# Low parts of 78 weight tiles computed in earlier feed-forward stages, stored to DRAM and loaded again

## The chip, the cores and the metric

The kernel runs on one core of a Trainium2 chip. The time is that of one execution on the device, in microseconds (us); three executions of the kernel before were taken.

## The reference

The model is a two-layer decoder trunk on 512 tokens of width 1024, in float32. Each layer adds half a SwiGLU feed-forward block (hidden width 2816), then a mixer, then half of a second feed-forward block. The mixer of layer 0 is the RWKV-7 time mixing (16 heads of 64, a recurrence over the tokens), that of layer 1 a causal convolution module.

```python
for i in range(DEPTH):
    x = x + 0.5 * swiglu(rms_norm(x, g[i, 0]), w_gate[i, 0], w_up[i, 0], w_down[i, 0])
    h = rms_norm(x, g[i, 1])
    x = x + (rwkv7_time_mix(h, ...) if i % 2 == 0 else conformer_conv(h, ...))
    x = x + 0.5 * swiglu(rms_norm(x, g[i, 2]), w_gate[i, 1], w_up[i, 1], w_down[i, 1])
return rms_norm(x, final_norm)
```

## The kernel before

All large products are products of a weight block of 128 x 128 with activations, channels on partitions and tokens along the free axis. For accuracy each float32 operand is split into a high part, its cast to the format F32R, and a low part, the rest. A product is then three matrix products: high by high, high by low, low by high (`mmw`).

The weights come as one stream of tiles, `wst`, eight blocks (512 KB) to a tile, in the order in which the steps of the program take them. `wfetch` handles tile i: SP loads it into `wr` (three buffers), ScalarE casts it to the high part `wh`, VectorE subtracts to get the low part `wl` (two buffers each). There are 446 tiles. `wblk` hands out the blocks and fetches one tile ahead.

`program()` lists the steps: `gu` and `dn` are the two halves of a feed-forward block, `f0` to `f3` the four blocks. Between `f0` and `f1` lies the time mixing: `rw` and `rx` norm the input, `kk`, `k`, `r`, `v`, `lora`, `w2`, `g1` are projections, `a` and `b` the two stages of a head group's recurrence, `w` the output projection. Between `f2` and `f3` lies the convolution: `cin` (input projection and gate), `tap` (31 taps, shared by VectorE in `dwa`, ScalarE and GpSimd in `dwt`, and TensorE in `dwx`, whose shifted inputs go through DRAM as `hd` and come back as `hr`), `cln` (layer norm), `co` (output projection). Some steps work on half of the tokens, 256 columns, some on all 512.

The steps don't issue instructions. They record them in `Sched`, which afterwards issues them by a list schedule: from modelled costs each engine takes, of the instructions whose operands and buffers are there, the one that can start first, and among equals the one that is oldest in program order (the casts of weights count as 10 us older, `LEAD`). SP, which issues the loads and stores, is scheduled in the same way. Working tiles of 2 KB a partition come from a pool of 80 slots. Where TensorE would idle for long, the schedule adds products that nothing reads (`warm`). In the profile all recorded instructions have one line, L617, where `emit` issues them; they are told apart by their tiles.

Up to 8 transfers of a queue are under way at a time: each waits for the semaphore of the eighth before it.

Of the kernel before, what the change touches and what calls it, by code (L numbers as in the profile page):

```python
# [12 lines left out]
F32 = mybir.dt.float32  # L13
F32R = mybir.dt.float32r
I32 = mybir.dt.int32
AF = mybir.ActivationFunctionType
ALU = mybir.AluOpType

P = 128
T = 512  # L20
D = 1024
NB = D // P
# [3 lines left out]
WT = 8  # L26
CH = 64
# [58 lines left out]
HALF3 = 1  # L86

# [5 lines left out]
def program():  # L93
    """The steps in program order (their weight blocks are streamed in this order). A step
    with a half h works on tokens 0-255 (0), 256-511 (1) or on all of them (2)."""
# [6 lines left out]
    def ffn(f, j0=0, mid=None):  # L102
        """From hidden block j0 on; with mid (lists of steps), the last sums run on one half of
        the tokens, then on the other half with one of the lists before each."""
# [74 lines left out]

PROG = program()  # L180

# [40 lines left out]
class Sched:  # L222
    """Records engine instructions in program order and issues them in the order of a
    list schedule: each engine takes the oldest instruction whose operands are there."""
# [50 lines left out]
    def after(self, eng, ap, n=1):  # L275
        """The next n instructions of an engine also wait for the writers of ap."""
        self.extra.append([eng, ap, n])
# [61 lines left out]
    def lag(a, b):  # L339
        """From the end of an instruction on a to the start of its reader on b."""  # L340
# [41 lines left out]
    def order(self):  # L382
# [38 lines left out]
        def fits(op, e):  # L421
            """Time at which the op's new tiles have room on engine e, or None."""
# [36 lines left out]
        def free(op, e):  # L459
            """Time from which no other engine's earlier instruction is at the op's banks."""  # L460
# [167 lines left out]
class Net:  # L628
    def __init__(self, ctx, tc, xT, wst, cvec, cst, dwv, outT):
# [17 lines left out]
        self.wtiles = {}  # L647
        self.wnext = 0
# [30 lines left out]
    def warm(self):  # L679
        """A product that nothing reads: keeps the tensor engine's clock up."""  # L680
# [6 lines left out]
    def wfetch(self):  # L687
# [8 lines left out]
        l = self.s.tile(self.wp, [P, WT, P], F32R, f"wl{i}", "wl", WB)  # L696
        self.s.lead = LEAD
# [4 lines left out]
        self.wtiles[i] = (h, l)  # L702

# [23 lines left out]
    def projs(self, ps, parts):  # L727
        """A projection of parts of the tokens: (columns, operand) each."""
# [17 lines left out]
    def turn(self, out, src):  # L746
        """Transposes each [P, P] block of src."""
# [4 lines left out]
    def scratch(self, name):  # L752
        """DRAM tile for a [P, NC, CH] array, strided so that the diagonal 16-blocks of a
        head lie at one stride: views (whole, low half, high half, blocks of head 0, 1)."""
# [6 lines left out]
    def rsqrt(self, y, v, n, tight=False):  # L761
        """y = v ** -0.5 elementwise on a small tile."""
# [37 lines left out]
    def sq_block(self, b, nm, h=2):  # L800
        """Sums the squares of x over its blocks but the last, on tokens of half h."""
# [891 lines left out]
```

## Time and profile before

| | |
|---|---|
| median of three runs | 2296.72 us (2292.44 to 2300.92) |
| the profiled execution | 2300.92 us, span 2300.8 us |
| TensorE products busy | 2214.8 us, 96% of the span |
| VectorE busy | 1368.3 us, 59% |
| ScalarE busy | 912.2 us, 40% |
| GpSimd busy | 608.6 us, 26% |
| low parts `wl` on VectorE | 561.5 us in 448 instructions |
| bytes moved | 261.96 MB, 114 GB/s on average |

Times in the profile count from the first instruction. PE is TensorE, PEld its loading of weights, DVE VectorE, ACT ScalarE, POOL GpSimd, SP the engine that issues most transfers. A view by windows gives each engine's busy time in a stretch, and the share of full speed that TensorE's clock was granted there. A view of waits names what ended an engine's idle time. The stages lie about so: first feed-forward block 0 to 390, time mixing 390 to 990 (with parts of the second feed-forward block in its gaps), rest of the second block to 1313, third block to 1681, convolution to about 1900 (with the start of the fourth block), fourth block to the end.

### The profile page before, as it was taken

The page shows a single profiled execution, that of the slowest core. Times are in us where ns is not written, and L with a number is a line of the kernel's source. Part 1 is how long each engine was busy: PE and PEld are TensorE (multiplying, and loading weights), DVE is VectorE, ACT ScalarE, POOL GpSimd, SP SyncE. Part 2 cuts the span into 40 slices and gives each one's busy share as a digit, 9 for nine tenths or more (in the row PEclk, how much of TensorE's full clock was granted, in tenths as well). Part 3 has the DMA queues.
Part 4 walks back from the last instruction along what each step waited for, and adds up shares of the span by engine and source line. Part 5 has one row for each costly group of instructions (what it writes and reads, how often), then busy time and mean ns, then how long its engine had stood idle before and what let it go on. Part 6 is the DMA issues. An engine that isn't in the chain of part 4 may idle for free. (4 is left out here: it accounts for less than half of the span.)

```text
span 2300.8 us, 37819 instructions
## 1 busy us (share of the span) xinstructions
PE 2214.8 (96%) x15256; PEld 1903.0 (83%) x15256; DVE 1368.3 (59%) x2201; ACT 912.2 (40%) x1506; POOL 608.6 (26%) x582
## 2 busy tenths in 40 slices
PE   9999999899989999999999999999997799999998
PEld 7888888667778788899999888888875589998898
DVE  5333347876796786566433433334479998753454
ACT  4222235546633453344322322123344555532343
POOL 2100113543352161022011112011157733311111
PEclk9999999899998997999999999999999999999999
DMA  4333336123224233256533333333334635653465
GB/s 154 97 96 101 97 124 183 46 75 90 60 64 115 76 101 98 76 166 182 156 93 92 92 98 99 92 101 93 92 111 124 164 98 166 179 147 93 126 184 158
DMA packets 120464, 261.96 MB, mean 114 GB/s; under 512 B 47072, under 2 KB 59744, under 8 KB 120288
## 3 DMA queue, kind: packets, MB, share of 16 engines
q1 hardware_dynamic: 86624, 254.29, 37.5%
q10 hardware_dynamic: 33664, 5.25, 1.3%
q8 instruction: 120, 1.97, 0.4%
q14 instruction: 56, 0.46, 0.1%
HBM read 249.96 MB, written 9.54 MB: 113 GB/s over the span
## 5 line engine op out<-in xcount | busy, mean ns | idle before, releaser
L617 ACT CAST wh<-wr 128x1024 fp32r<-128x1024 f32 (+1 forms) x448 | 467.3, 1045 | 994.3 <-issue 365.3
L617 DVE TENSOR_TENSOR wl<-wr,wh 128x1024 fp32r<-128x1024 f32 (+1 forms) x448 | 561.5, 1255 | 254.3 <-ACT wh L617 245.9
L617 DVE SCALAR_TENSOR_TENSOR dwa<-ch,dw,dwa 128x256 f32<-128x256 f32 (+10 forms) x176 | 115.3, 697 | 0.1
L617 POOL TENSOR_TENSOR f1ss<-f1ss,n1rs 128x256 f32<-128x256 f32 (+1 forms) x33 | 47.2, 1433 | 235.6 <-ACT f1ss L617 235.5
L617 POOL TENSOR_TENSOR f0ss<-f0ss,n0rs 128x512 f32<-128x512 f32 x22 | 38.6, 1756 | 258.0 <-ACT f0ss L617 258.0
L617 POOL TENSOR_TENSOR f2ss<-f2ss,n2rs 128x512 f32<-128x512 f32 x22 | 39.0, 1773 | 255.8 <-ACT f2ss L617 255.8
L617 POOL TENSOR_TENSOR f3ss<-f3ss,n3rs 128x256 f32<-128x256 f32 (+1 forms) x33 | 49.3, 1495 | 182.5 <-ACT f3ss L617 182.5
L617 PE MATMUL f3u<-f_h,wl 128*128 128x256 f32 (+1 forms) x264 | 84.7, 321 | 2.1 <-DVE wl L617 2.1
L617 PE MATMUL f3g<-f_h,wl 128*128 128x256 f32 (+1 forms) x264 | 84.8, 321 | 1.5 <-DVE wl L617 1.4
L617 PE MATMUL f3u<-f_l,wh 128*128 128x256 f32 (+1 forms) x264 | 84.5, 320 | 0.0
L617 PE MATMUL f3g<-f_l,wh 128*128 128x256 f32 (+1 forms) x264 | 84.3, 319 | 0.0
L617 PE MATMUL f3g<-f_h,wh 128*128 128x256 f32 (+1 forms) x264 | 84.2, 319 | 0.0
L617 PE MATMUL f3u<-f_h,wh 128*128 128x256 f32 (+1 forms) x264 | 84.2, 319 | 0.0
L617 POOL TENSOR_TENSOR dwt<-dwt,dwt 128x256 f32<-128x256 f32 (+5 forms) x80 | 72.9, 923 | 2.7
L617 PE MATMUL f0g<-f_2h,wh 128*128 128x512 f32 x176 | 70.2, 399 | 2.5 <-ACT wh L617 2.5
L617 PE MATMUL f0g<-f_2l,wh 128*128 128x512 f32 x176 | 70.1, 399 | 1.9 <-DVE f_2l L617 1.9
L617 PE MATMUL f2g<-f_2h,wl 128*128 128x512 f32 x176 | 69.4, 394 | 0.0
L617 PE MATMUL f0u<-f_2h,wh 128*128 128x512 f32 x176 | 69.4, 394 | 0.0
L617 PE MATMUL f0g<-f_2h,wl 128*128 128x512 f32 x176 | 69.4, 394 | 0.0
L617 PE MATMUL f0u<-f_2l,wh 128*128 128x512 f32 x176 | 69.4, 394 | 0.0
L617 PE MATMUL f2u<-f_2l,wh 128*128 128x512 f32 x176 | 69.4, 394 | 0.0
L617 PE MATMUL f2g<-f_2l,wh 128*128 128x512 f32 x176 | 69.3, 394 | 0.0
(1509 smaller groups left out, 7048.7 us busy)
## 6 DMA issues: line engine op xcount, KB each, us to landing
wr<-wst SPq DMA_DIRECT2D x444, 512.0 KB, 3.6
hr<-hd SPq DMA_DIRECT2D x64, 64.5 KB, 3.8
hr<-hd SPq DMA_DIRECT2D x64, 59.2 KB, 2.0
x<-xT SPq DMA_DIRECT2D x8, 256.0 KB, 6.1
xspill<-x SPq DMA_DIRECT2D x8, 256.0 KB, 4.4
dl<-Gb ACTq DMA_DIRECT2D x16, 128.0 KB, 2.1
t<-dt ACTq DMA_DIRECT2D x8, 256.0 KB, 3.4
xr<-xspill SPq DMA_DIRECT2D x8, 256.0 KB, 6.0
```

Source lines behind the costliest of these rows:

```text
L617: self.tc.keep_in_program_order(getattr(eng, m)(*op.args, **op.kw))
```

## The change

78 tiles are taken out of the usual path: the tiles 77 to 124, which the time mixing takes first, and 300 to 329, the convolution's. For each of them a new step `ps` is put into the program earlier: the 48 of the time mixing spread over the first feed-forward block from its third hidden block on, the 30 of the convolution over the third feed-forward block (`early`; `WCOUNT` counts the weight blocks of a step). `step_ps` loads the raw tile in two halves of 256 KB (`pw`), casts each on ScalarE (`ph`), subtracts on VectorE in place, and stores the low part to DRAM (`lo`). When such a tile comes up later, `wfetch` loads the raw tile as before and casts it on ScalarE, but loads the low part from DRAM into `wl` in place of VectorE's subtraction. Nothing else of the computation changes. (In the new file the docstrings and comments are gone, so the line of the recorded instructions is L658.)

```diff
+PS = (48, 30)
...
+def early(prog, of, to, at, end, n, skip=0):
+    pos = [0]
+    for s in prog:
+        pos.append(pos[-1] + WCOUNT(*s))
+    lo, hi = -(-pos[of] // WT), pos[to] // WT
+    tiles = list(range(lo, hi))[skip:skip + n]
+    a, b = pos[at], pos[end]
+    where = {}
+    for k, i in enumerate(tiles):
+        p = a + (b - a) * (k + 0.5) / len(tiles)
+        j = at
+        while pos[j + 1] <= p:
+            j += 1
+        where.setdefault(j, []).append(("ps", i))
+    out = []
+    for j, s in enumerate(prog):
+        out += [s] + where.get(j, [])
+    return out, set(tiles)
...
 PROG = program()
+PRE = set()
+PROG, t_ = early(PROG, find(PROG, "rw", 1), find(PROG, "prep", 1, 1), 3, find(PROG, "rw", 0), PS[0])
+PRE |= t_
+PROG, t_ = early(PROG, find(PROG, "conv"), find(PROG, "cln", 1), find(PROG, "prep", 2) + 2, find(PROG, "conv"), PS[1])
+PRE |= t_
...
         l = self.s.tile(self.wp, [P, WT, P], F32R, f"wl{i}", "wl", WB)
+        if i in self.lows:
+            nc.sync.dma_start(l.bitcast(F32), self.lows[i].rearrange("p (a b) -> p a b", b=P))
+            self.s.lead = LEAD
+            nc.scalar.copy(h, raw)
+            self.s.lead = 0.0
+            self.wtiles[i] = (h, l)
+            return
...
+    def step_ps(self, i):
+
+        nc = self.nc
+        self.lows[i] = d = self.dp.tile([P, WT * P], F32, name=f"lo{i}")
+        for k in range(WT * P // T):
+            c = slice(k * T, k * T + T)
+            n = T // P
+            w = self.slot(f"pw{i}_{k}", F32R)
+            h = self.slot(f"ph{i}_{k}", F32R)
+            nc.sync.dma_start(w.bitcast(F32).rearrange("p (a b) -> p a b", b=P), self.wst[i][:, k * n:k * n + n])
+            nc.scalar.copy(h, w.bitcast(F32))
+            nc.vector.tensor_tensor(w, w.bitcast(F32), h.bitcast(F32), ALU.subtract)
+            nc.sync.dma_start(d[:, c], w.bitcast(F32))
```

How the schedule places the new instructions shows in the built order. The number after a name's letters is the tile, the last number a buffer's.

On SP in the first feed-forward block, before: nothing but raw tiles, one after the other.

```order
L617 DMA wr7_154<-wst 128x1024
L617 DMA wr8_158<-wst 128x1024
L617 DMA wr9_166<-wst 128x1024
L617 DMA wr10_170<-wst 128x1024
L617 DMA wr11_178<-wst 128x1024
L617 DMA wr12_182<-wst 128x1024
```

Now, from raw tile 8 on:

```order
L658 DMA wr8_168<-wst 128x1024
L658 DMA lo87_275<-pw87_0_276 128x512
L658 DMA lo88_292<-pw88_0_293 128x512
L658 DMA pw101_0_435<-wst 128x512
L658 DMA lo78_158<-pw78_1_161 128x512
L658 DMA wr9_181<-wst 128x1024
L658 DMA lo89_309<-pw89_0_310 128x512
L658 DMA lo90_314<-pw90_0_315 128x512
L658 DMA lo79_175<-pw79_1_178 128x512
L658 DMA pw101_1_437<-wst 128x512
L658 DMA lo91_326<-pw91_0_327 128x512
L658 DMA lo80_192<-pw80_1_195 128x512
```

Between two raw tiles stand the loads of tiles that are wanted some 90 tiles later, and the stores of low parts. Up to and with raw tile 16 SP's queue has 78 `pw` loads, 62 `lo` stores and 17 raw tiles.

On VectorE in the convolution, where the gate of channel block 4 (`ctg4`) is scaled, before:

```order
L617 TENSOR_TENSOR ctg4_2_2685<-cg4_2_2680,ncrs_2593 128x512
L617 TENSOR_TENSOR wl311_2699<-wr311_2697,wh311_2698 128x1024
L617 SCALAR_TENSOR_TENSOR dwa3_2667<-ch3_2666,dw_2562,dwa3_2667 128x246
L617 SCALAR_TENSOR_TENSOR ch4_2686<-cta4_2_2684,vec_72,ctg4_2_2685 128x512
L617 SCALAR_TENSOR_TENSOR dwa3_2667<-ch3_2666,dw_2562,dwa3_2667 128x245
L617 TENSOR_SCALAR dwa4_2687<-ch4_2686,dw_2562,vec_72 128x256
```

Now:

```order
L658 TENSOR_TENSOR ctg4_2_3075<-cg4_2_3070,ncrs_2983 128x512
L658 SCALAR_TENSOR_TENSOR dwa3_3057<-ch3_3056,dw_2952,dwa3_3057 128x256 x2
L658 SCALAR_TENSOR_TENSOR ch4_3076<-cta4_2_3074,vec_72,ctg4_2_3075 128x512
L658 SCALAR_TENSOR_TENSOR dwa3_3057<-ch3_3056,dw_2952,dwa3_3057 128x256
L658 TENSOR_SCALAR dwa4_3077<-ch4_3076,dw_2952,vec_72 128x256
```

The subtraction `wl311` between the taps `dwa` is gone; the taps of block 3 that stood around it now stand around `ch4` alone.

On SP in the time mixing, before:

```order
L617 DMA wr94_850<-wst 128x1024
L617 DMA wr95_860<-wst 128x1024
L617 DMA wr96_866<-wst 128x1024
L617 DMA wr97_894<-wst 128x1024
L617 DMA wr98_901<-wst 128x1024
```

Now:

```order
L658 DMA wr96_1106<-wst 128x1024
L658 DMA wl94_1092<-lo94_356 128x1024
L658 DMA wr97_1134<-wst 128x1024
L658 DMA wl95_1102<-lo95_365 128x1024
L658 DMA wr98_1141<-wst 128x1024
L658 DMA wl96_1108<-lo96_377 128x1024
L658 DMA wr99_1164<-wst 128x1024
```

Each raw tile is followed by the low part of the tile two before it. In the convolution such low parts stand between the groups of small transfers `hd` and `hr`.

## Rows read from the trace of the kernel before

**Rows 1.** The page: span, and busy us (share of the span) xinstructions.

```profile
span 2300.8 us, 37819 instructions
PE 2214.8 (96%) x15256; PEld 1903.0 (83%) x15256; DVE 1368.3 (59%) x2201; ACT 912.2 (40%) x1506; POOL 608.6 (26%) x582
```

**Rows 2.** Windows by stage: length, busy us by engine, granted clock (1.00 full), DMA share, GB/s.

```profile
core 0: us, PE busy (x) PEld busy (x) DVE busy (x) ACT busy (x) POOL busy (x), PEclk, DMA share, GB/s
0.00:8.00 8.00, 4.80 (x13) 3.51 (x13) 0.75 (x1) 2.85 (x4) 0.41 (x5) 0.98 0.64 198
8.00:16.00 8.00, 7.76 (x27) 5.94 (x28) 7.42 (x9) 8.00 (x15) 3.59 (x3) 0.80 1.03 408
146.00:322.00 176.00, 176.00 (x761) 142.66 (x760) 63.97 (x71) 44.18 (x54) 19.83 (x11) 1.00 0.34 99
395.00:450.00 55.00, 42.09 (x181) 31.24 (x181) 55.00 (x66) 29.58 (x55) 34.67 (x23) 0.89 0.14 44
630.00:690.00 60.00, 52.32 (x597) 42.73 (x597) 55.17 (x130) 23.76 (x55) 30.43 (x44) 0.94 0.24 61
1720.00:1900.00 180.00, 149.11 (x1071) 116.37 (x1072) 176.01 (x289) 85.44 (x168) 109.64 (x117) 0.91 0.48 130
```

**Rows 3.** Windows: the third feed-forward stage.

```profile
1313.00:1681.00 368.00, 368.00 (x1598) 298.58 (x1597) 148.05 (x165) 103.33 (x127) 59.58 (x42) 1.00 0.32 94
```

**Rows 4.** TensorE's waits, 1720 to 1900: us in total, times, longest.

```profile
PE ca L617 <- DVE wl L617: 12.4, 5, 3.7
PE cg L617 <- DVE wl L617: 7.6, 4, 4.6
PE co L617 <- DVE wl L617: 0.8, 2, 0.4
```

**Rows 5.** VectorE by groups, 1720 to 1900: busy us, mean ns | idle before.

```profile
L617 DVE SCALAR_TENSOR_TENSOR dwa<-ch,dw,dwa 128x256 f32<-128x256 f32 (+10 forms) x147 | 97.2, 705 | 0.0
L617 DVE TENSOR_TENSOR wl<-wr,wh 128x1024 fp32r<-128x1024 f32 x28 | 38.4, 1372 | 0.1
```

**Rows 6.** TensorE's waits, 395 to 1000.

```profile
PE v L617 <- DVE wl L617: 1.4, 3, 0.6
PE k L617 <- DVE wl L617: 0.5, 1, 0.5
```

**Rows 7.** VectorE by groups, 395 to 450, then 630 to 690.

```profile
L617 DVE TENSOR_TENSOR wl<-wr,wh 128x1024 fp32r<-128x1024 f32 x4 | 4.8, 1212 | 0.0
...
L617 DVE TENSOR_TENSOR wl<-wr,wh 128x1024 fp32r<-128x1024 f32 x5 | 6.4, 1284 | 0.8 <-ACT wh L617 0.7
```

**Rows 8.** DMA issues: engine, count, KB each, median us from issue to landing.

```profile
wr<-wst SPq DMA_DIRECT2D x444, 512.0 KB, 3.6
x<-xT SPq DMA_DIRECT2D x8, 256.0 KB, 6.1
xspill<-x SPq DMA_DIRECT2D x8, 256.0 KB, 4.4
cst<-cst SPq DMA_DIRECT2D x1, 849.0 KB, 6.7
vec<-cvec SPq DMA_DIRECT2D x1, 104.0 KB, 1.9
```

**Rows 9.** ScalarE in order of time, 20 to 105: start, us, what.

```profile
21.18 1.05 ACT L617 CAST wh<-wr 128x1024 fp32r<-128x1024 f32 x1 [3.44 <-PE f0g L617]
...
99.38 1.05 ACT L617 CAST wh<-wr 128x1024 fp32r<-128x1024 f32 x1 [3.96 <-PE f0g L617]
104.94 1.05 ACT L617 CAST wh<-wr 128x1024 fp32r<-128x1024 f32 x1 [3.98 <-issue]
```

**Rows 10.** TensorE by groups, 1681 to 1925.

```profile
L617 PE MATMUL dwx<-hr,dg 128*32 128x256 f32 (+3 forms) x384 | 31.1, 406 | 0.1
```

**Rows 11.** VectorE and ScalarE by groups and shapes, 0 to 330.

```profile
L617 DVE TENSOR_TENSOR wl<-wr,wh 128x1024 fp32r<-128x1024 f32 x57 | 69.8, 1225 | 41.1 <-ACT wh L617 38.2
L617 DVE TENSOR_TENSOR f0h4l<-f0gs,f0h4h 128x512 fp32r<-128x512 f32 x1 | 0.7, 687 | 0.0
...
L617 ACT CAST f0h10h<-f0gs 128x512 fp32r<-128x512 f32 x1 | 0.6, 624 | 0.0
```

More of the change, by code (lines that the diff above doesn't have):

```diff
@@ L177, in program, with WCOUNT, find @@
     return out
-PROG = program()
+def early(prog, of, to, at, end, n, skip=0):
[16 more added lines that the diff above has]
+    return out, set(tiles)
+def WCOUNT(kind, *a):
+    return {"gu": lambda: 16, "dn": lambda: len(a[1]), "kk": lambda: NB * len(a),
+            "kh": lambda: NB * (len(a) - 1), "k": lambda: NB, "r": lambda: NB, "v": lambda: NB,
+            "lora": lambda: NB, "w2": lambda: 1, "g1": lambda: 2 * NB, "a": lambda: 2,
+            "b": lambda: 4, "w": lambda: a[2][1] - a[2][0], "cin": lambda: 2 * NB,
+            "co": lambda: NB}.get(kind, lambda: 0)()
+def find(prog, *s):
+    return next(i for i, x in enumerate(prog) if x[:len(s)] == s)
+PROG = program()
+PRE = set()
[3 more added lines that the diff above has]
+PRE |= t_
 def constants():
@@ L647, in __init__ @@
         self.wtiles = {}
+        self.lows = {}
         self.wnext = 0
```

## The prediction

> **What bounds the kernel now.** I read the page first. TensorE is busy for 2214.8 of 2300.8 us, 96%, VectorE for 59% [rows 1], so the whole can gain at most about 86 us of idle TensorE plus what a low clock costs. The windows by stage come next, because the average hides three kinds of stage. In the feed-forward stages TensorE has no idle time at all: 176.00 of 176.00 us in the first, 368.00 of 368.00 in the third, with VectorE under half busy [rows 2, 3]. In the convolution (1720 to 1900) it is the other way round: VectorE is busy for 176.01 of 180 us, TensorE for 149.11 at a granted clock of 0.91 [rows 2]. The time mixing has two such stretches: 395 to 450 (VectorE 55.00 of 55, TensorE 42.09) and 630 to 690 (55.17 of 60, TensorE 52.32) [rows 2].
>
> Then the waits of TensorE in the convolution: of 31 us of idle time, 12.4 + 7.6 + 0.8 = 20.8 us end with VectorE's `wl`, the low part of a weight tile [rows 4]. There VectorE has 28 such subtractions at 1372 ns, 38.4 us, beside the taps of the convolution (97.2 us) [rows 5]. In the time mixing TensorE waits for `wl` directly for only 0.5 and 1.4 us in the projections `k` and `v` [rows 6]; there VectorE's queue delays other things.
>
> **The change, first part: what is taken away.** The tiles 77 to 124 and 300 to 329 lose their subtraction, 78 of 448. In the convolution the first eight of the thirty are subtracted before 1720, so 22 of the 28 go: 22 x 1.372 = 30 us of VectorE. That is the upper bound, if VectorE alone set the end. With 146 us left to it there, TensorE's 149 us (136 at full clock) bound about as much, so I take the waits that vanish by name: **-21 us**; the lower bound is 0 (a rival below). In the time mixing only the two bound stretches count: 4 subtractions of 4.8 us and 5 of 6.4 us [rows 7], **-11 us**, bounds 0 and the 20.6 us for which TensorE idles there [rows 2]. Elsewhere VectorE has room, and I cost what is removed at nothing.
>
> **Second part: what replaces it at the use.** Each of the 78 tiles gets a second transfer of 512 KB into `wl`. It can only start when TensorE has released the buffer, two tiles back, and such a transfer takes 3.6 us to land [rows 8]. Before, the same release was followed by the cast (1.05 us [rows 9]) and the subtraction (1.37 us [rows 5]): 2.4 us. A full tile occupies TensorE for 5.56 us (104.94 - 99.38, two casts paced by TensorE [rows 9]), which covers 3.6. The twelve half-width tiles of the convolution (318 to 329) occupy it for half, 2.8 us: 0.8 us late each if nothing else lies between, 10 us at most, 0 at least. I take **+3**, near the low end, since the order leaves products of other steps between most of them. SP issues the raw tile two ahead before each `wl` tile, so the raw tiles aren't held up behind that wait; the small transfers of the taps do stand behind it, and I cost that at nothing, since TensorE's tap products `dwx` waited 0.1 us in all [rows 10]; with that cover gone it is some of the 3 us above.
>
> **Third part: the early computation, where the program order is not what is run.** Program order spreads the 48 tiles over the first feed-forward stage. The list schedule doesn't: SP takes whatever can start, and the raw tiles wait for their three buffers while `pw` transfers wait for nothing but free slots. In SP's order, up to and with the raw tile 16, stand 78 `pw` loads and 62 `lo` stores of 256 KB, 17 raw tiles of 512 KB, and the inputs (8 x 256 KB, 849 KB, 104 KB) [rows 8]: 20.4 + 16.3 + 8.9 + 3.1 = 48.7 MB. By 16 us the kernel had moved 8 x 198 + 8 x 408 = 4,850 KB [rows 2], and 408 GB/s, with the 16 engines' share at 1.03, is the only row here where the engines are full. If that rate holds, the other 43.85 MB take 107.5 us, and tile 16 lands at 16 + 107.5 + 2.3 (3.6 us to landing less 1.3 us of moving) = 125.8 us. Its cast ran at 99.38 before (the fifteenth whole tile, the first at 21.18) [rows 9]; TensorE turned to the tile 5.56 us later, and cast and subtraction need 2.3 us, so it must land by 102.6. **+23 us** of TensorE waiting, which cannot be won back, since TensorE had no idle time there. After tile 16 the order thins out and the lag shrinks. A TensorE that pauses also loses clock: 0.91 was granted in the convolution, at 83% busy [rows 2]. 9% of some 50 us of work is 5 us, most of it inside the wait for transfers: I take **+2**, bounds 0 and 5.
>
> VectorE can just do its share there: 78 subtractions of 687 ns [rows 11] are 53.6 us. Its own load in 146 to 322 is 63.97 of 176 us, 36% [rows 2], so it has 57 us free between 16 and 105 us and would be on time; if its first `pw` comes only at 25 us, 51 us are free and it is 3 us late, inside the 23. ScalarE has 78 casts of 0.62 us [rows 11] and more room. Both take their queues in order, so a late `pw` holds a cast of a raw tile behind it; that is the same lag, not another one.
>
> In the third feed-forward stage the slots are fuller, and SP's order has no more than about one early tile for each raw one: 3 x 524 KB in 5.56 us is 283 GB/s, under 408, and VectorE goes from 148 to about 190 of 368 us [rows 3]. I take 0.
>
> **The sum.** 23 + 2 + 3 - 21 - 11 = -4 us, against the profiled execution's own 2300.92 us (span 2300.8 [rows 1]): 2297. The median of the three runs, 2296.72, lies 4 us under that execution, so I forecast **2293 us**. A measurement of this kernel can tell about 0.5%, 11.5 us, from no change: this is no change.
>
> **The rivals.**
> *Slower: mixed traffic moves slower than the opening burst.* The burst held only loads; here a third are stores to DRAM. While a feed-forward stage streams alone, a share of 0.34 moves 99 GB/s, 291 GB/s for a full share [rows 2]. At that rate tile 16 lands at 16 + 150.7 + 2.3 = 169, 66 us late: 66 + 2 + 3 - 32 = +39, **2336 us**. The place is the same stall in the first feed-forward stage. It decides from 357 GB/s down: there the lag is 38.5 us and the total 11.5 us up. For it: nothing in the trace shows stores under load (the spill of x, 256 KB, takes 4.4 us to land [rows 8]). Against: the loads of x, also 256 KB, were among those that moved at 408 GB/s. Chance 0.20.
> The Trainium skill, "DMA: Bandwidth & Descriptors", section "Where 436 GB/s comes from", says that the HBM side binds at about 358 GB/s for a core; an estimate by that figure makes tile 16 38 us late and the total 2308, at the edge of this rival. The 408 GB/s over 8 us [rows 2] stand against it, and the measurement decides.
>
> *Faster: stores ride beside loads.* If the two directions don't share a limit, 27.6 MB of loads remain after 16 us, 67.7 us at 408 GB/s: tile 16 lands at 86, in time, and only VectorE's 3 us remain. 3 + 3 - 32 = -26, **2271 us**. For it: loads and stores go opposite ways; against: the share counts each engine busy whatever it moves. Chance 0.30, as it also stands for a time mixing that gives more than 11 us (its clock is 0.89 in the first bound stretch).
>
> *The transfer takes the place of the subtraction.* If `wl` lands as late as VectorE had it done, TensorE's 20.8 us of waits only change their name, the time mixing likewise, and the stall remains: +25, **2322 us**. For it: 3.6 us against 2.4. Against: 5.56 us of cover for full tiles. Chance 0.10.
>
> That the change doesn't do what it says can be left out: the built order has 78 `wl` loads on SP and 78 fewer `wl` subtractions on VectorE.
>
> **How the numbers follow.** The forecast has 0.40, with 2276 to 2312 as its own range (a stall of 15 to 33 us, gains of 20 to 42); 0.07 of it lies under 2285 and 0.02 over 2308. Faster by over 0.5%: 0.30 + 0.07 = 0.37. Within: 0.31. Slower: 0.20 + 0.10 + 0.02 = 0.32. The range goes from 2264, just under the fast rival, to 2330, over the third and into the slow one, half of which it leaves out; with the fast rival's tail that is under 2 in 10.
>
> **What would show it.** Right: from about 50 to 130 us a DMA share near 1 and TensorE waiting for `wh` or `wl`, some 23 us in all, and the first feed-forward stage ending that much later; from 1681 on, scaled, VectorE off its limit and the stage about 18 us shorter; the entry of the time mixing shorter by some 5 us. Wrong: no stall (then the DMA share stays under 1 with stores in flight, and the fast rival holds), a moving rate under 357 GB/s at a share of 1 (the slow one), or waits of TensorE for `wl` transfers in the convolution near 20 us.

## The result and the profile after

The changed kernel takes **2375.51 us** (median of four runs, 2372.82 to 2378.65); the kernel before took 2298.59 us in the same comparison. The ratio is 1.0331, with a 95% interval of 1.0302 to 1.036: slower by 77 us, where 2293 us and no change had been forecast. The time lies outside the forecast range of 2264 to 2330 us. The page of the changed kernel answers to [rows 1]:

```profile
span 2374.3 us, 38916 instructions
PE 2242.8 (94%) x15281; PEld 1920.2 (81%) x15281; DVE 1393.9 (59%) x2303; ACT 992.7 (42%) x1638; POOL 586.8 (25%) x582
```

VectorE is not relieved overall, it has 26 us more: a subtraction that is moved is still done, in two halves, which cost 118 us where the 78 whole ones had taken 106. TensorE has 28 us more of busy time for the same products, 7 of them in the schedule's filling products (`warm`, 25.9 us before and 32.9 now). Where the 73.5 us between the two profiled executions lie is read from the first products of four stages (timelines of TensorE by tile; us from the start of the span):

| | before | after | stretch before | stretch after | difference | forecast |
|---|---|---|---|---|---|---|
| last group of down products, `f0d`, of the first block starts | 321.9 | 375.2 | 321.9 | 375.2 | +53.3 | +25 |
| third block, `f2g` | 1312.8 | 1385.9 | 990.9 | 1010.7 | +19.8 | -11 |
| convolution, `ca` | 1681.5 | 1755.4 | 368.7 | 369.5 | +0.8 | 0 |
| fourth block, `f3d` | 2163.5 | 2236.6 | 482.0 | 481.2 | -0.8 | -18 |

(The stretch of the last line, from `ca` to `f3d`, takes in the gate and up products of the fourth block. The +3 of the second part is put with the convolution, for whose tiles it was worked out.) A trace is one execution, and executions of one kernel differ: in e1's comparison those of the kernel before lie between 2285.86 and 2314.15 us. So a few us between two stretches may be chance, and where medians and stretches differ, the medians decide. Windows of the changed kernel, as in [rows 2, 3]:

```profile
core 0: us, PE busy (x) PEld busy (x) DVE busy (x) ACT busy (x) POOL busy (x), PEclk, DMA share, GB/s
16.00:60.00 44.00, 28.59 (x126) 21.98 (x126) 28.36 (x44) 23.46 (x41) 8.43 (x6) 0.86 1.05 397
60.00:146.00 86.00, 64.91 (x233) 48.69 (x233) 55.53 (x78) 40.59 (x68) 10.16 (x5) 0.86 0.92 327
146.00:322.00 176.00, 174.46 (x751) 140.53 (x750) 79.07 (x91) 55.29 (x74) 18.93 (x23) 1.00 0.53 167
...
1386.00:1755.00 369.00, 369.00 (x1600) 299.04 (x1599) 162.07 (x186) 116.85 (x149) 61.15 (x42) 1.00 0.43 129
1790.00:1970.00 180.00, 147.10 (x1023) 114.42 (x1022) 158.88 (x294) 92.85 (x192) 110.15 (x133) 0.88 0.64 191
```

In the first two rows TensorE is busy for 93.5 of 130 us at a granted clock of 0.86 while the transfers run at a share of 1.05 and then 0.92. From 146 on nearly nothing is lost, and the third block has its TensorE full as before. The last row is the convolution, shifted by 70 us (its first product moved by 74): VectorE has been taken from 176 to 159 of 180 us, and TensorE did no more for it, 147 against 149.

The waits of TensorE from 0 to 400 (us in total, times, longest):

```profile
PE f0u L658 <- ACT wh L658: 22.6, 4, 13.4
PE f0g L658 <- ACT wh L658: 7.8, 2, 6.4
PE f0g L658 <- DVE wl L658: 3.5, 4, 1.5
PE f0u L658 <- DVE wl L658: 3.5, 4, 1.0
```

The largest, 13.4 us before 57.39, is for the cast of raw tile 5. ScalarE in order of time shows what that cast stood behind:

```profile
38.76 0.62 ACT L658 CAST ph<-pw 128x512 fp32r<-128x512 f32 x1
42.48 0.62 ACT L658 CAST ph<-pw 128x512 fp32r<-128x512 f32 x1 [3.10 <-DMA lo<-pw]
...
54.22 2.18 ACT L658 CAST ph<-pw 128x512 fp32r<-128x512 f32 x4 [9.04 <-DMA lo<-pw]
56.30 1.04 ACT L658 CAST wh<-wr 128x1024 fp32r<-128x1024 f32 x1
```

Raw tile 5 was issued at 30.08 and landed at 36.06; the transfer eight places behind it, which needs that landing, was issued at 36.13. Its cast ran at 56.30 (38.27 before): not the tile was late, but the `ph` ahead of it, whose slot was held by a low part that had not been stored yet. Every later tile for whose cast TensorE waited over 1 us in this stall had landed long before: tiles 7, 8, 11 and 13 landed at 51.69, 63.81, 95.67 and 114.27, and their casts ran at 70.84, 85.63, 110.50 and 130.26, 15 to 22 us later. A late cast also releases its raw buffer late: raw tile 8 was issued at 58.62, just after tile 5's subtraction had ended at 58.60. And the clock, in the windows around this wait:

```profile
40.00:50.00 10.00, 3.98 (x18) 2.86 (x16) 4.90 (x8) 2.70 (x5) 0.00 (x0) 0.87 1.05 402
50.00:60.00 10.00, 2.57 (x5) 1.66 (x6) 4.53 (x7) 5.79 (x11) 0.00 (x0) 0.50 1.05 399
60.00:70.00 10.00, 10.00 (x42) 8.03 (x42) 8.82 (x15) 5.88 (x11) 3.95 (x1) 0.95 1.01 371
```

After the pause the granted clock is 0.50, the lower level of 1.2 GHz, so what TensorE then does takes longer too.

### The profile page after: what moved, and what is told of

It is laid out like the page before. It is cut to its first block, busy times and chain, and to the rows that moved or that the text cites. A ratio compares the mean times of both kernels' runs of the same rounds, so it can differ in the third digit from the quotient of the medians.

```text
span 2374.3 us, 38916 instructions
## 1 busy us (share of the span) xinstructions
PE 2242.8 (94%) x15281; PEld 1920.2 (81%) x15281; DVE 1393.9 (59%) x2303; ACT 992.7 (42%) x1638; POOL 586.8 (25%) x582
## 5 line engine op out<-in xcount | busy, mean ns | idle before, releaser
L658 ACT CAST wh<-wr 128x1024 fp32r<-128x1024 f32 (+1 forms) x448 | 467.2, 1044 | 890.6 <-issue 344.3
L658 DVE TENSOR_TENSOR wl<-wr,wh 128x1024 fp32r<-128x1024 f32 (+1 forms) x370 | 455.7, 1232 | 228.4 <-ACT wh L658 221.6
L658 DVE TENSOR_TENSOR pw<-pw,ph 128x512 fp32r<-128x512 f32 x156 | 112.2, 757 | 22.4 <-ACT ph L658 21.8
L658 POOL TENSOR_TENSOR f0ss<-f0ss,n0rs 128x512 f32<-128x512 f32 x22 | 39.1, 1781 | 310.4 <-ACT f0ss L658 298.7
L658 DVE SCALAR_TENSOR_TENSOR dwa<-ch,dw,dwa 128x256 f32<-128x256 f32 (+11 forms) x176 | 114.7, 695 | 0.8
L658 POOL TENSOR_TENSOR f1ss<-f1ss,n1rs 128x256 f32<-128x256 f32 (+1 forms) x33 | 49.8, 1509 | 241.5 <-ACT f1ss L658 241.4
L658 ACT CAST ph<-pw 128x512 fp32r<-128x512 f32 x156 | 89.9, 616 | 39.6 <-DMA pw<-wst 27.0
L658 POOL TENSOR_TENSOR f2ss<-f2ss,n2rs 128x512 f32<-128x512 f32 x22 | 39.1, 1778 | 256.7 <-ACT f2ss L658 256.7
L658 POOL TENSOR_TENSOR f3ss<-f3ss,n3rs 128x256 f32<-128x256 f32 (+1 forms) x33 | 51.4, 1557 | 194.0 <-ACT f3ss L658 186.9
L658 PE MATMUL f0u<-f_2h,wh 128*128 128x512 f32 x176 | 73.2, 416 | 22.6 <-ACT wh L658 22.6
L658 PE MATMUL f3u<-f_h,wh 128*128 128x256 f32 (+1 forms) x264 | 84.6, 320 | 2.3 <-ACT wh L658 2.3
L658 PE MATMUL f3g<-f_h,wl 128*128 128x256 f32 (+1 forms) x264 | 85.1, 322 | 0.1
L658 PE MATMUL f3g<-f_h,wh 128*128 128x256 f32 (+1 forms) x264 | 84.6, 320 | 0.0
L658 PE MATMUL f3u<-f_h,wl 128*128 128x256 f32 (+1 forms) x264 | 84.4, 320 | 0.0
L658 PE MATMUL f3g<-f_l,wh 128*128 128x256 f32 (+1 forms) x264 | 84.4, 320 | 0.0
L658 PE MATMUL f3u<-f_l,wh 128*128 128x256 f32 (+1 forms) x264 | 84.2, 319 | 0.0
L658 PE MATMUL f0g<-f_2h,wh 128*128 128x512 f32 x176 | 70.6, 401 | 7.8 <-ACT wh L658 7.8
L658 PE MATMUL f0u<-f_2h,wl 128*128 128x512 f32 x176 | 72.8, 414 | 3.5 <-DVE wl L658 3.5
L658 PE MATMUL f0g<-f_2h,wl 128*128 128x512 f32 x176 | 70.6, 401 | 3.5 <-DVE wl L658 3.5
L658 PE MATMUL f0g<-f_2l,wh 128*128 128x512 f32 x176 | 70.9, 403 | 2.4 <-DVE f_2l L658 2.4
L658 PE MATMUL f0u<-f_2l,wh 128*128 128x512 f32 x176 | 72.3, 411 | 0.0
L658 PE MATMUL f2g<-f_2h,wl 128*128 128x512 f32 x176 | 69.5, 395 | 0.0
```

The lines of the kernel that those rows point to most:

```text
L658: self.tc.keep_in_program_order(getattr(eng, m)(*op.args, **op.kw))
```

## The experiments

Times are medians; the ratio is to the kernel before on the same chip. "Idle" below is the time of a stretch less TensorE's busy time in it, and filling products are the schedule's own `warm`. Lines left out of an edit are marked `...`.

### The first feed-forward block

**Early work in step with the raw tiles** (e1_paced). SP may take up an early load only behind the cast of the newest raw tile:

```diff
+            self.s.after("sync", self.wtiles[self.wnext - 1][0])
             nc.sync.dma_start(w.bitcast(F32)...)
```

> The changed kernel with one edit: each early load also waits for the cast of the weight tile that was fetched last before it in program order, so the 48 early tiles are spread over the first feed-forward block (first load after raw tile 8, about one early tile per raw tile). Theory Q (the order of the queues makes the stall: early work let loose ahead of the raw tiles): the first feed-forward block ends within 5 us of the kernel before (first product of its second sums near 322 to 327 us, 375 in the changed kernel), total near 2320 us, as only the 20 us of the time mixing stay. Theory W (the work itself, its bytes and subtractions, is too much for the block): at least 30 us of the 53 remain, total 2350 us or more.

Measured: 2320.29 us (2317.35 to 2321.24), ratio 1.0103 [1.0067, 1.0139]. The last down product starts at 321.1. The window from 16 us to it:

```profile
16.00:321.10 305.10, 303.53 (x1320) 246.07 (x1321) 163.36 (x212) 121.38 (x176) 44.76 (x38) 1.00 0.72 226
```

VectorE does 44 us more there than before the change (163 for 120) and the transfers carry 226 GB/s (98 before), and TensorE is idle for 1.6 of 305.1 us. So the 53 us come from the order of the early work, not from its amount. By the medians 27 us of slowdown remain (the two traces differ by 15), and they lie elsewhere.

**`ph` from its own buffers** (e5_own_ph), so that it never waits for a store:

```diff
-            h = self.slot(f"ph{i}_{k}", F32R)
+            h = self.s.tile(self.wp, [P, T], F32R, f"ph{i}_{k}", "ph", 2)
```

> The changed kernel with one edit: the high parts of the early tiles (ph) come from two buffers of their own, and not from the slot that the low parts take in turn. The order of transfers is the changed kernel's. Theory B (buffer): the first feed-forward block lost 53 us because a ph waits on in-order ScalarE for the store of the low part that had its buffer, with the raw tiles' casts behind it; without that wait only the share of the mixed transfers is left, about 23 us, so the block's last down product starts near 345 us (375 in the changed kernel, 322 before) and the kernel takes 2340 to 2350 us. Theory C (transfers): the block waits for data throughout, and a ph that comes earlier changes nothing; the last down product starts at 367 us or later and the kernel takes 2365 us or more.

Measured: 2366.02 us (2363.45 to 2369.01), ratio 1.0308 [1.0251, 1.0366]; `f0d` starts at 366.2, 9 us earlier than in the changed kernel. That is C's end of the scale: I had built the whole surplus on the wait for a buffer, and what goes with it here is 9 us, about as long as the one wait of 9.04 us shown above. But C's claim, that the block waits for data throughout, doesn't hold either: ScalarE's queue still delays raw tiles that are there. Raw tile 8 went out on SP at 59.57 and landed at 65.33 (no raw tile of the first 200 us took more than 8.7 us); its cast, the second row of ScalarE's here, ran 12 us after that:

```profile
76.53 1.22 ACT L658 CAST ph<-pw 128x512 fp32r<-128x512 f32 x2 [0.59 <-DVE pw L658]
77.66 1.04 ACT L658 CAST wh<-wr 128x1024 fp32r<-128x1024 f32 x1
```

Ahead of it stood `ph` casts, with waits for VectorE of 17.7 us in 25 places up to 160 us. The changed kernel has no such waits: two buffers bring them, since a `ph` must wait for the subtraction two before it. So the 9 us are what this edit gains, and what more buffers would gain was not tried.

**Without the stores** (e8_no_store): only the first early tile is stored; the others load that tile's low part at their use.

```diff
-        self.lows[i] = d = self.dp.tile(...)
+        self.lows[i] = d = next(iter(self.lows.values())) if self.lows else self.dp.tile(...)
...
-            nc.sync.dma_start(d[:, c], w.bitcast(F32))
+            if len(self.lows) == 1:
+                nc.sync.dma_start(d[:, c], w.bitcast(F32))
```

> The changed kernel with the stores of the low parts left out but for the first tile's two; at their use all 78 tiles load that one stored tile, so the low parts of 77 tiles are wrong. The early loads, casts and subtractions stay. In this order raw tile 8 has 22.5 MB up to and with it, and after it come raw tiles alone: at 397 GB/s it lands near 62 us, some 8 us late, and nothing after it is late by transfers. Theory T (transfers): the stall of 53 us was the queue of loads and stores; here 5 to 12 us are left and the last down product starts at 327 to 334 us. Theory Q (queue of ScalarE): the casts of raw tiles stand in order behind the casts of early pieces, which wait for VectorE, whatever the transfers do; with 54 early pieces ahead of raw tile 8 the stall is 20 us or more and the last down product starts at 342 us or later.

Measured in one run: 2317.01 us; `f0d` starts at 337.0, 15 us late, between the two theories. The windows tell why:

```profile
40.00:50.00 10.00, 6.57 (x23) 4.56 (x22) 8.88 (x12) 4.65 (x8) 1.60 (x1) 0.81 1.05 395
50.00:60.00 10.00, 10.00 (x38) 7.97 (x37) 1.39 (x2) 0.62 (x1) 0.00 (x0) 0.85 1.05 396
60.00:70.00 10.00, 7.62 (x27) 5.79 (x26) 2.15 (x2) 1.56 (x2) 1.27 (x1) 0.83 0.34 124
70.00:80.00 10.00, 7.74 (x33) 5.67 (x32) 3.74 (x4) 2.52 (x3) 0.00 (x0) 1.00 0.30 103
```

Idle time is 3.4 + 2.4 + 2.3 us, and the transfers are through by 60 us. The 8 us equal theory T's term, but not by its mechanism. Raw tile 8 did land when T has it, at 61.92, but its cast ran at 72.83. The tiles for whose casts TensorE waited, 5, 7 and 8, had all landed 8 to 11 us before these ran. ScalarE's queue held the last two, and not with `ph`, as theory Q has it, but with the block's own gate, in the order that the schedule had fixed from its modelled transfers:

```profile
61.86 0.63 ACT L658 ACTIVATE f0ss<-f0gs 128x512 f32<-128x512 f32 x1 [4.93 <-DVE f0gs L658]
62.39 1.03 ACT L658 CAST wh<-wr 128x1024 fp32r<-128x1024 f32 x1
72.30 0.62 ACT L658 CAST f0h3h<-f0gs 128x512 fp32r<-128x512 f32 x1 [8.88 <-DVE f0gs L658]
72.83 1.99 ACT L658 CAST wh<-wr 128x1024 fp32r<-128x1024 f32 x2
```

The other 7 us are slow and filling products. The same split (idle and busy time by windows from 16 us to `f0d`, the fillers from the same window for `warm`) holds in all of them:

| 16 us to `f0d` | idle | filling products | real products | `f0d` starts |
|---|---|---|---|---|
| before | 1.9 | 0 | 304.0 | 321.9 |
| after | 38.1 | 4.3 | 316.8 | 375.2 |
| own `ph` buffers | 29.2 | 4.8 | 316.2 | 366.2 |
| no stores | 9.9 | 2.3 | 308.8 | 337.0 |

Of the 53 us, 36 are idle time, 4 filling products, and 13 are real products at a lower clock. Of the idle time, 9 us go with the wait for slots; most of the rest goes with the stores, since 8 us are left without them. Whether by their bytes or by SP's order the runs don't tell: between 16 and 160 us SP waited 26.3 us for VectorE's subtraction of a piece before it could store it, with raw tiles behind, and without stores both are gone (and in that order the early loads ahead of raw tile 16 are also fewer, 54 for 78).

### The time mixing

**Without cost** (e3_free): the high part stands in for the low part of the 78 tiles; there is no early work and no transfer.

```diff
-PROG, t_ = early(...)
+_, t_ = early(...)
...
-        l = self.s.tile(self.wp, [P, WT, P], F32R, f"wl{i}", "wl", WB)
-        if i in self.lows:
-            nc.sync.dma_start(l.bitcast(F32), self.lows[i]...)
+        l = None if i in PRE else self.s.tile(self.wp, [P, WT, P], F32R, f"wl{i}", "wl", WB)
+        if i in PRE:
+            l = h
```

> No early steps and no second transfers: for the 78 tiles the high part stands in for the low part as well, so neither VectorE nor the queues do anything for it (the computation leaves out the low parts of these weights). It measures the most that the change could win at the place of use. Theory A (the transfers take back what VectorE gives): gains of 25 to 40 us, 2260 to 2275 us. Theory B (VectorE's subtraction is not what sets these stages; the next wait in line takes over): less than 12 us gained, 2287 to 2299 us.

Measured: 2279.95 us (2273.53 to 2286.55), ratio 0.993 [0.9908, 0.9951], between the two theories. The stretch from `f0d` to `f2g` takes 976.9 us, 14 less than before; the one from `ca` to `f3d` 472.9, 9 less; by the medians the whole kernel gains 14, since the traced execution of the kernel before is the slowest of the four that gave its 2298.59 us. **With the transfers alone** (e4_transfer): one tile is computed early, and all 78 load its low part.

```diff
-        if i in self.lows:
-            nc.sync.dma_start(l.bitcast(F32), self.lows[i]...)
+        if i in PRE:
+            nc.sync.dma_start(l.bitcast(F32), next(iter(self.lows.values()))...)
```

> As the run with free low parts, but each of the 78 tiles loads its low part by a transfer of 512 KB, all from the one stored tile (one early tile in all; the low parts of the other 77 are that tile's, not their own). It adds the transfers at the use, and nothing in the feed-forward blocks. Theory A: the gain of the free run is lost, 2295 to 2320 us, 30 us or more above it. Theory B: within 10 us of the free run.

Measured: 2318.84 us (2315.82 to 2320.05), ratio 1.0097 [1.006, 1.0133]: 39 us above the free kernel, as Theory A has it. The whole slowdown that pacing left is in the transfers at the use; the early work, once paced, costs nothing (2320 against 2319). By stretch, the time mixing takes 1006.7 us, 30 more than free; the convolution 482.6, 10 more. One execution doesn't fit: e8 loads the same 48 low parts in the time mixing, which took 989.5 us there, no longer than before, against 1004.5 to 1010.7 in the changed kernel, e1, e4 and e5. Its idle and filling time, 55.3 us, is like theirs (52.3 to 64.6; 50.2 before), but its real products took 934.2 us, theirs 942.1 to 956.1. It was run once, so whether that is chance stays open.

**Which tiles** (e7_paced20, e11_paced_half28). The early tiles of the time mixing are of two kinds. The first 20 (77 to 96) are multiplied with all 512 tokens (two of them in halves), the other 28 (97 to 124) with 256. Both kernels are paced and leave the convolution as it was:

```diff
-PS = (48, 30)
+PS = (20, 0)
```

> The paced kernel with 20 early tiles only, all of them full-width ones of the time mixing, and none of its half-width tiles and of the convolution. Theory H (half-width): what costs time in the time mixing is that a half-width tile's low part is as long in transfer as VectorE took to compute it, or longer, for half the products; without them the time mixing takes no longer than before, 980 to 991 us, and the kernel 2280 to 2296 us. Theory Q (load in general): each stored tile costs; with 20 of 48 the time mixing still takes 996 us or more, and the kernel 2298 us or more.

```diff
-PS = (48, 30)
+PS = (28, 0)
...
-PROG, t_ = early(..., find(PROG, "rw", 0), PS[0])
+PROG, t_ = early(..., find(PROG, "rw", 0), PS[0], 20)
```

> The paced kernel with the other 28 early tiles of the time mixing alone, those that are multiplied with 256 columns (97 to 124), and none of the first 20 and of the convolution. Theory H (half-width): these are the tiles that cost time, since a transfer takes as long as TensorE needs for such a tile and waits for its buffer; the time mixing takes 1000 us or more (991 before, 983.5 with the 20 full-width tiles alone, 1004.5 with all 48), and the kernel 2303 to 2316 us. Theory N (number): each early tile does a little harm whatever its width, and the 20 gained by chance of their place; then 28 lie between, at 988 to 996 us, and the kernel takes 2290 to 2302 us.

Measured: the 20 full ones 2289.45 us (2286.97 to 2296.3), ratio 0.9977 [0.9953, 1.0]; the 28 half ones 2305.73 us (2300.58 to 2313.85), ratio 1.003 [1.0, 1.006]. The time mixing in one window each, first the 20, then the 28:

```profile
321.10:1304.60 983.50, 950.02 (x8279) 838.96 (x8278) 638.77 (x1231) 440.47 (x804) 281.53 (x295) 0.96 0.41 122
```

```profile
321.20:1323.30 1002.10, 959.12 (x8285) 844.75 (x8284) 637.72 (x1238) 441.91 (x795) 280.83 (x295) 0.96 0.41 125
```

With VectorE relieved of 20 tiles the stretch is 7.4 us shorter than before, with 28 others 11.2 longer, and idle and filling time there goes from 50.2 us before to 43.5 and 56.7. That is as theory H has it both ways; Q and N have the stretches wrong. But the stretches are of executions 6 and 8 us slower than their medians, and by the ratios the two kernels lie 0.2% under and 0.3% over the kernel before, with intervals that reach to 1.0. The 28 tiles also differ in place: most stand between the steps of the recurrence. So the half-width tiles are the likely cause; that it is their width and not their place is not shown.

**A third buffer** (e6_paced_third_wl; e10_paced20_third_wl with 20 tiles), so that a low part's transfer can start a tile earlier:

```diff
-        l = self.s.tile(self.wp, [P, WT, P], F32R, f"wl{i}", "wl", WB)
+        l = self.s.tile(self.wp, [P, WT, P], F32R, f"wl{i}", "wl", 3)
```

> The paced kernel (early tiles only as far as the raw tiles leave room) with a third buffer for the low parts at their use, so that their transfer can start a tile earlier. Theory L (late start): the time mixing lost 14 us and the convolution gained nothing since a low part's transfer starts only when a buffer comes free and lands late; with a third buffer the time mixing takes 991 us or less and the kernel 2290 to 2302 us. Theory Q (load): the time goes in the load that 78 more transfers put on SP's queue and on the transfers beside them, and an earlier start changes no more than 5 us: 2315 us or more.

> The paced kernel with 20 early tiles (full-width ones of the time mixing alone) and a third buffer for the low parts. Theory L: a transfer that can start a tile earlier gave the paced kernel with 78 tiles 16 us; with 20 tiles there is a quarter of it, 4 us, on top of what 20 tiles gave: 2283 to 2287 us, faster than the kernel before by about 0.4%. Theory H: what was gained by the third buffer was the half-width tiles' share alone, and 20 full-width tiles have no use for it: 2288 to 2292 us.

Measured: 2304.03 us (2292.6 to 2310.94), ratio 1.0028 [1.0001, 1.0055] for all 78, 16 us faster than with two buffers; 2290.88 us (2288.23 to 2296.76), ratio 0.997 [0.9949, 0.999] for the 20, by the ratios 1.6 us faster than with two, and 1.1 us shorter in the time mixing, which is nearer H's nothing than L's 4 us but doesn't exclude them. So the buffer helps where half-width tiles are loaded, and little or not at all where they aren't. Theory L is short of its full price for the 78, though: the time mixing took 998.8 us (it wanted 991 or less), in an execution 7 us slower than the median. Idle and filling time there came back to 50.0 us, from 58.2 with two buffers (50.2 before, 63.3 in the changed kernel); what stays are real products at 948.8 us against 940.7, and no run tells their cause apart from the clock (0.95 and 0.96 granted).

What SP waits for in the stretch of the `v` products, before (568 to 740) and after (625 to 831), shows the mechanism:

```profile
SPq L617 <- DVE wl L617: 105.2, 14, 17.4
SPq L617 <- DVE mv L617: 33.0, 3, 12.4
...
SPq L617 <- PE v L617: 0.2, 1, 0.2
```

```profile
SPq L658 <- PE v L658: 71.3, 12, 12.1
SPq L658 <- PE g L658: 35.1, 3, 17.2
SPq L658 <- ACT wh L658: 25.4, 13, 13.5
```

Before, SP waited for VectorE's subtraction to release a raw buffer. Now it waits for TensorE itself to release a `wl` buffer, and the next raw tile and all else on SP stand behind that. The transfer then takes 3.5 us to land (median of 78), while a half-width tile keeps TensorE for 2.8 (half of the 5.56 us of a full one). The stretch has grown from 172.1 to 205.2 us. Of TensorE's waits in it, only a few carry the name of the new transfer:

```profile
PE X L658 <- DMA t<-dt: 7.2, 2, 4.9
...
PE v L658 <- DMA wl<-lo: 1.2, 1, 1.2
```

`t<-dt` is a small round trip through DRAM in the recurrence, on ScalarE's queue: 3.4 us to land before, 5.4 now. So the lateness seems to come out at what the recurrence needs next; that it runs through `t<-dt` is not shown by a run.

### The convolution

**The 30 tiles of the convolution alone** (e2_conv_only):

```diff
-PS = (48, 30)
+PS = (0, 30)
```

> The changed kernel with 30 early tiles for the convolution alone, none for the time mixing. Both theories on the stall: no stall in the first feed-forward block. Theory R (the convolution's waits only change their name, as in the changed kernel, where the stage kept its length): 2296 to 2304 us, within 0.3% of before. Theory S (the convolution does gain its 20 us, but in the changed kernel something from the earlier stages, as slots or buffers, takes it back): 2275 to 2285 us.

Measured: 2305.33 us (2293.97 to 2318.36), ratio 1.0045 [1.0011, 1.008], a microsecond over theory R's range; by the ratio 0.45% over the kernel before, where R had within 0.3%. S is out. The stretch from `ca` to `f3d` takes 485.5 us, 3.5 more than before. Over all traces it takes 480.5 to 485.5 us where the 30 low parts are loaded (the changed kernel, e1, e2, e4, e5, e6, e8) and 481.7 to 482.5 where the convolution is as it was (before, e7, e10, e11): no gain from 30 subtractions less.

**Free, with a third buffer for the high parts** (e9_free_third_wh). In the free kernel TensorE's waits for `wl` had turned into waits for `wh`. To that kernel's edit comes:

```diff
-        h = self.s.tile(self.wp, [P, WT, P], F32R, f"wh{i}", "wh", WB)
+        h = self.s.tile(self.wp, [P, WT, P], F32R, f"wh{i}", "wh", 3)
```

> The kernel that leaves the low parts of the 78 tiles out (the high part stands in, no early work, no transfer) with a third buffer for the high parts, so that a cast on ScalarE may stand a tile earlier. Theory S (ScalarE): with VectorE's part gone, the convolution gained only 9 us of the forecast 21 since the casts come late in ScalarE's order, behind the casts of the taps, and their buffers bound them; with a third buffer the stretch from the convolution's first product to the last down product falls to 465 us or less (473 without, 482 before). Theory D (VectorE): the taps on VectorE set the convolution's pace whatever the weights do; it stays at 470 to 476 us.

Measured: 2284.1 us (2279.88 to 2287.39), ratio 0.9942 [0.9921, 0.9963]; the stretch 475.0 us. TensorE's longest waits, 1660 to 1980 in the free kernel, then with the third buffer:

```profile
PE ca L658 <- ACT wh L658: 21.2, 5, 5.3
PE lnm L658 <- DVE dwa L658: 6.5, 2, 4.0
```

```profile
PE dwx L658 <- DMA hr<-hd: 11.2, 3, 5.1
PE lnm L658 <- POOL lns L658: 8.2, 1, 8.2
PE lnm L658 <- DVE dwa L658: 5.6, 2, 4.5
PE cg L658 <- ACT wh L658: 3.8, 1, 3.8
```

Theory S falls. The wait for `wh` goes from 21.2 to 3.8 us and others come up in its place; TensorE's idle time in the stretch is 35.6 us free and 35.1 with the buffer (34.7 before, 33.1 after). The filling products belong with it, and there the kernels differ: these are the `warm` products of the stretch, before and free.

```profile
1681.50:2163.50 482.00, 5.64 (x11) 2.84 (x11) 0.97 0.47 134
1668.00:2140.90 472.90, 0.00 (x0) 0.00 (x0) 0.96 0.46 136
```

Idle and filling time together is 40.3 us before, 39.4 after, 35.6 free and 35.4 with the buffer. So most of the 20.8 us that were named `wl` only change their name: without the subtractions 5 us go, and with the buffer nothing more. The other 4 us of the free kernel's 9 are real products that ran faster (441.7 us before, 437.4 free).

**Free, with three of VectorE's taps left out** (e12_free_fewer_taps), again on top of the free kernel's edit:

```diff
-        for j in range(1, nd):
+        for j in range(1, nd - 3):
             o, i = io(j)
             nc.vector.scalar_tensor_tensor(acc[:, o], h[:, i], w(j), acc[:, o], ALU.mult, ALU.add)
```

> The kernel that leaves the low parts of the 78 tiles out, with 3 of VectorE's 11 added taps left out as well, 48 instructions of 0.70 us, 33 us of VectorE. Theory D (VectorE): the first part of the convolution is paced by the taps on VectorE, so TensorE's idle time of 35 us there, which stayed the same without the subtractions and with a third buffer, now falls by 15 us or more, and the stretch from the convolution's first product to the last down product, 473 us, falls to 458 us or less. Theory C (chain): the pace is the chain through one channel block (gate, sigmoid on ScalarE, taps of ScalarE and GpSimd), and VectorE is full only because it finds work; the stretch falls by 5 us at most, to 468 us or more.

Measured: 2269.33 us (2265.84 to 2277.22), ratio 0.9871 [0.9839, 0.9903]. The stretch takes 460.5 us, 12 less, between the theories but nearer D's 458 than C's 468; idle time falls by 10 us to 25.7, where D asked for 15. All of it lies ahead of the first `co` product. The rows of the parts ahead of it and behind it, in the free kernel and with the taps left out, read:

```profile
1668.00:1833.30 165.30, 134.78 (x877) 103.10 (x875) 152.30 (x269) 81.03 (x162) 109.24 (x127) 0.90 0.48 129
1833.30:2140.90 307.60, 302.57 (x2041) 275.26 (x2042) 175.82 (x265) 137.32 (x220) 77.68 (x60) 0.99 0.45 139
```

```profile
1669.70:1822.90 153.20, 132.16 (x877) 100.75 (x875) 131.67 (x221) 81.69 (x162) 106.17 (x127) 0.93 0.52 140
1822.90:2130.20 307.30, 302.68 (x2041) 275.92 (x2042) 176.41 (x265) 137.68 (x219) 77.91 (x60) 0.99 0.46 139
```

In the second part TensorE is busy for 98% in both, so little can be gained there. In the first, 21 us less of VectorE go with 12 us less of time. VectorE's groups in the first part show what became of the subtractions, before and in the changed kernel:

```profile
L617 DVE SCALAR_TENSOR_TENSOR dwa<-ch,dw,dwa 128x256 f32<-128x256 f32 (+10 forms) x140 | 97.2, 742 | 0.0
L617 DVE TENSOR_TENSOR wl<-wr,wh 128x1024 fp32r<-128x1024 f32 x21 | 28.2, 1344 | 0.4 <-ACT wh L617 0.4
```

```profile
L658 DVE SCALAR_TENSOR_TENSOR dwa<-ch,dw,dwa 128x256 f32<-128x256 f32 (+11 forms) x170 | 111.4, 701 | 0.7
```

21 subtractions, 28.2 us, are gone from the part, and 30 taps, 14.2 us, have come into it from the second part, where they had been hidden under TensorE. VectorE is still the fullest engine: 150.97 of 168.7 us. So it sets at least part of the pace there; theory C's chain may set the rest.

## Why the prediction was wrong

**Third part, +23 and +2, measured +53: the stall is there, but the step from the transfers to TensorE failed.** The bytes were right, and so was the rate at first: with stores in the mix the transfers moved 397 GB/s at a share of 1.05 from 16 to 60 us, so the slower rival (291 GB/s) and the faster one (stores ride free) both fall. The Trainium skill, "HBM Reference", section "Specifications (TRN2)", gives about 425 GB/s for a core that streams alone, bounded by its 16 DMA engines, beside the per-core share of about 358; the 402 GB/s at full share lie over the second and 5% under the first, with loads and stores mixed.

Then two sentences failed. The first is "that is the same lag, not another one", which put the wait for casts in ScalarE's queue at nothing beside the transfers' lag. Raw tile 16 was to land at 125.8 us and be cast at once; it landed at 140.62, and its cast ran at 152.33, 53 us later than before (99.38). For a `ph` that waits, and the gates behind it, hold back the casts of raw tiles that have landed; the raw buffers come free late, SP stands behind them and behind subtractions, and the rate doesn't hold: 327 GB/s at a share of 0.92 from 60 to 146 us. With `ph` in its own buffers tile 16 landed at 129.62, near the forecast, its cast ran at 141.31, and the block was still 44 us late. The idle time came to 36 us in place of 23, and 4 us of filling products to it; 9 us of the idle time go with the wait for slots (e5). The second sentence is the +2 for the clock with its bounds of 0 and 5, taken from the convolution's mean of 0.91, where TensorE's pauses are short: real products alone took 13 us longer, in windows granted 0.50 to 0.96. e8 agrees with the way of reckoning the landing (tile 8 near 62 us, measured 61.92); that its idle time is also 8 us is luck, since TensorE waited there for casts of tiles that had landed.

**Second part, +3: the step that overlooked most, the transfers of the time mixing.** It priced a half-width tile (2.8 us on TensorE against 3.6 to land) and then counted twelve, those of the convolution from 318 on. Half-width are there 18, since the input projection's last four steps, tiles 312 to 319, work on half of the tokens too; and in the time mixing the 28 tiles of `v`, of the output projection and of what lies between are of the same kind, with the recurrence between them. These 28 it put at nothing. With all 48 the time mixing lost 20 us in the changed kernel and 14 when paced; e4 against e3 shows that it is the transfers (30 us there). By e7 and e11 the full-width tiles gain 7 and the half-width ones lose 11, which together is less than the 14 of all 48; what the rest is stays open. The term for what is taken away there, -11, was about right: by the traces the free kernel gains 14 in the stretch, 11 of it idle and filling time.

**First part, -21 in the convolution, measured -1 with the +3 of the second part: wrong.** It added up TensorE's waits for `wl` by name [rows 4]. The runs show that the name goes and most of the time stays: idle and filling time is 40.3, 39.4, 35.6 and 35.4 us before, after, free, and free with a third buffer. Upper and lower bound had been named as 30 and 0 (the upper one is 33: by the trace six of the thirty tiles, not eight, were subtracted before 1720); free of all cost the gain is 9, and the transfers at the use take that back (e2, e4). The rival "the transfer takes the place of the subtraction" comes nearest in this stage, though by waits for the cast on ScalarE, 14.0 us in the changed kernel, and not for the transfer, 1.8.

**Third feed-forward stage, 0: right**, 369 us against 369 [rows 3], with 120 transfers more, at 129 GB/s far under the limit.

Summed in the forecast's own terms, by the traces: the first block 53 for 25, time mixing +20 for -11, third block +1 for 0, convolution -1 for -18. That makes the 73 us between the two traced executions, for a forecast of -4; the medians differ by 77.

## What to carry to other kernels

Work that is moved into a stage with free engines is not free if it enters the same in-order queues as the stage's own stream: pace it by that stream, since a list schedule takes whatever is ready first; here that one line is worth the 53 us of the first block. A wait's name tells who came last, not what an engine's relief is worth: leave the work out altogether once, without paying for it, and see whether idle time falls, filling products counted with it, before building the replacement; here that bound was 14 us in all. And before a transfer stands in for computation, compare how long a tile lasts on TensorE with how long the transfer takes from the release of its buffer: where it is shorter, time went here, and a third buffer gave back 16 us. The 20 full-width tiles are the best version found, 2289.45 us, 0.2% under the kernel before (0.3% with the third buffer), less than its runs differ among themselves.

## What the runs showed of the hardware

Loads and stores between DRAM and the core share one limit of about 400 GB/s: 402 at a share of 1.05 with loads and stores mixed, 395 and 396 at 1.05 for loads alone in e8, 408 at 1.03 in the opening burst [rows 2]. I hadn't expected how much a pause costs beyond itself: after 13.4 us without products the granted clock was 0.50, and the mean of the next 10 us window was 0.95. In this block 36 us of idle time came with another 13 us of slow products, and 8 us with 5 in the kernel without stores. The Trainium skill, "TensorE: Matmul & The Clock Gate", section "Part 1: The HAM clock gate (the "warmup" mystery)", says that an idle array falls back to half its clock; the rows agree.
